# Sums over partitions by transposes and a VectorE sum, and identity products as transposes, in a two-layer hybrid decoder kernel

## The chip, the cores and the metric

The kernel runs on one core of one Trainium2 chip. The metric is the device time of one execution in microseconds (us). Three timed runs of the kernel before took 2297.41, 2301.21 and 2301.37 us, so the median is 2301.21 us.

Five engines matter. TensorE (PE in the profile, with its weight loads listed apart as PEld) multiplies matrices and writes to PSUM. VectorE (DVE) and ScalarE (ACT) do elementwise work and read PSUM. GpSimd (POOL) hardly works here. SyncE (SP) issues the transfers (DMA). Each engine takes its instructions in the order in which they were written into its queue.

## The reference, cut to what matters

Two decoder layers run over 1024 tokens of width 1024. Layer 0 has sparse attention, layer 1 a gated short convolution, and each is followed by a SwiGLU FFN. Everything is float32.

```python
c_act = jax.nn.silu(c)
for i in range(DEPTH):
    mod = c_act @ ada_w[i] + ada_b[i]
    sh1, sc1, g1, sh2, sc2, g2 = [m[:, None, :] for m in jnp.split(mod, 6, axis=-1)]
    h = _rmsnorm(x, norm1_g[i]) * (1.0 + sc1) + sh1
    ...                       # y = sparse attention (i = 0) or short convolution (i = 1) of h
    x = x + g1 * y
    h = _rmsnorm(x, norm2_g[i]) * (1.0 + sc2) + sh2
    x = x + g2 * _swiglu(h, ffn_w_gate[i], ffn_w_up[i], ffn_w_down[i])
return x
```

Three small things inside it are what the change touches: the vector-matrix product `c_act @ ada_w[i]` that gives the twelve conditioning vectors of 1024 values (six per layer), the sum of squares of each token in `_rmsnorm`, and the division by a per-token number (the norm's root, the key norm, the softmax's sum).

## The kernel before, in words

Activations lie transposed on the chip: features on the 128 partitions, tokens along the free side, in two halves of 512 tokens. A per-token number is therefore needed on every partition, and a sum over features is a sum over partitions.

**Large products.** Each float32 operand is split into a high and a low part (`whi`, `wlo`; ScalarE casts, VectorE subtracts), and every product is three matmuls, 128x128 weights against 512 columns (`mm3`). The FFN and the convolution's products use a two-by-two scheme with seven products instead of eight. Accumulators are PSUM banks of 128x512 float32: tags `mm` (2 banks), `g` (5 banks, in the part after attention), `o` (1), `L` (2 of two banks each, in attention) and `sm` (1 bank).

**Conditioning vectors.** `ada_step` multiplies a 128-row piece of `ada_w` by the 128 matching values of `c_act`, one per partition, and adds it into an accumulator (`acc` and `sc` for the first two vectors of layer 0, `adacc` for the others, 512 columns at a time). After eight pieces the accumulator has to be summed over its 128 partitions and turned so that a feature lies on a partition: `ada_end` does this with one float32 matmul per 128 columns, the accumulator as weights against a column of ones (`self.ones`), and VectorE adds `ada_b`. The first two vectors are made before the first norm. Ten halves (five vectors) are made during attention, eight during the first FFN, two during the second.

**Norms.** `norm_stat` squares x on ScalarE, adds the eight pieces on VectorE, and sums over partitions with four matmuls against ones, so that a token lies on a partition. `norm_bc` takes the root of 4 values per partition (`rsqrt_small`: VectorE, ScalarE, VectorE) and spreads them back: four float32 products with the identity, the weights being one value per partition repeated along 128 columns. The result is a 128x512 bank in which each partition has the norm factors of 512 tokens. There are six such statistics behind attention; the first norm of all gets its sums from ScalarE and uses `norm_bc` only.

**Attention.** For each block of 128 queries and each of 4 key groups: scores on PE into `ps_L`, mask and maximum on VectorE, exponent on ScalarE, transposes of the weights on PE (`p` against the identity, into an `mm` or `sm` bank), copies on ScalarE or VectorE (`pf`), values on PE into `ps_o`. `group_end` then divides by the softmax's sum: the reciprocal is repeated along 128 columns (`rw`) and turned by two products with the identity. `k_out` does the same for the key norm with four (`rb`), twice in all.

**What sets the order.** No engine order is written by hand. All calls are recorded with a priority, an estimate of their duration (`Plan.cost`) and their dependences, and `Plan.drain` writes them out engine by engine, as a list scheduler: whichever engine is free first takes the ready operation of the best priority. So an operation with another estimate can shift its neighbours. A tile of a tag with one buffer (`sm`) is handed on when all operations on the former tile are done. In the estimates a `transpose` counts 0.107 us of PE, and a float32 matmul with up to 128 columns 0.213 us.

In the profile every instruction has line 244 (the one place where recorded calls are written out), so tile names tell them apart.

Of the kernel before, what the change touches and what calls it, by code (L numbers as in the profile page):

```python
# [9 lines left out]
F32 = mybir.dt.float32  # L10
# [5 lines left out]
ALU = mybir.AluOpType  # L16
AX = mybir.AxisListType
# [433 lines left out]
P = 128  # L451
T = 1024
D = 1024
KT = D // P
TB = T // P
HW = 512
# [26 lines left out]
def blk(b):  # L483
    return slice(b * P, (b + 1) * P)


class Trunk:
# [97 lines left out]
    def setup(self, c, positions, ada_b, n1, n2, conv_w, gq, gk, lg, lb, rope_c, arenas, kgb, freq):  # L585
        nc, cp = self.nc, self.cp
# [3 lines left out]
                                fill=0.0, base=0, channel_multiplier=1)  # L590
        self.ones = cp.tile([P, 1], F32, name="ones")
        nc.vector.memset(self.ones, 1.0)
        self.blk4 = cp.tile([P, 4], F32, name="blk4")
# [57 lines left out]
    def ada_end(self, layer, j, lhs, half=0):  # L651

        nc = self.nc
        ps = self.ps("sm")
        n = 0
        for v in lhs:
            for c in range(0, v.free, P):
                nc.tensor.matmul(ps[:, n:n + 1], v[:, c:c + P], self.ones, start=True, stop=True)
                n += 1
        dst = self.mod[layer][j]  # L660
        c0 = half * 4
        b0 = layer * 48 + j * 8 + c0
        nc.vector.tensor_tensor(dst[:, c0:c0 + n], ps[:, 0:n], self.adab[:, b0:b0 + n],
                                op=ALU.add)
        if j in (1, 4) and c0 + n == KT:
            self.ada_scale(layer, j)
# [11 lines left out]
    def norm_bc(self, ss, sp, tag):  # L678
        nc = self.nc
# [3 lines left out]
        bc = self.ps(tag)  # L683
        for t in range(4):
            nc.tensor.matmul(bc[:, blk(t)], r[:, t:t + 1].to_broadcast([P, P]),
                             self.ident, start=True, stop=True)
        return bc
# [108 lines left out]
class Attention:  # L796
# [281 lines left out]
    def k_out(self, ab, rk, half, sl):  # L1078
# [5 lines left out]
        for i in range(4):  # L1084
            nc.tensor.matmul(bc[:, blk(i)], rb[:, blk(i)], tk.ident, start=True, stop=True)
        for two in range(2):
# [232 lines left out]
    def group_end(self, b, g, ops, sums):  # L1319
# [8 lines left out]
        for i in range(2):  # L1328
            nc.tensor.matmul(bc[:, blk(i)], rw[:, blk(i)], tk.ident, start=True, stop=True)
        on = sp.tile([P, 2, P], F32, name="on", tag="on")  # L1330
# [24 lines left out]
class Tail:  # L1355
# [57 lines left out]
    def norm_stat(self, half, tag="sm"):  # L1413
# [3 lines left out]
        for d in range(KT):  # L1417
# [4 lines left out]
            acc = sq  # L1422
        ss = self.tk.ps(tag)
        for t in range(4):
            nc.tensor.matmul(ss[:, t:t + 1], acc[:, blk(t)], self.tk.ones, start=True, stop=True)
        return self.tk.norm_bc(ss[:, 0:4], self.up, tag)

# [448 lines left out]
```

## Time and profile before

| | us |
|---|---|
| timed runs, lowest / median / highest | 2297.41 / 2301.21 / 2301.37 |
| profiled execution, span from first to last instruction | 2296.5 |
| PE busy | 2229.7 (97%), 11659 matmul instructions |
| VectorE busy | 1896.1 (83%), 3821 instructions |
| ScalarE busy | 1126.0 (49%), 2139 instructions |
| mean granted TensorE clock | 0.989 |

For the profiled execution only the span is recorded; the median of the timed runs lies 4.7 us (0.2%) above it. Differences worked out from the trace are made against the span and then set against the median.

PE is recorded as busy from an instruction's start to its result, and consecutive matmuls overlap, so the distance between starts tells what a matmul takes of the queue, and its duration does not. VectorE's and ScalarE's rows overlap a little too.

### The profile page before, as it was taken

How to read it: one execution, taken by the hardware profiler on the slowest of the kernel's cores; microseconds unless marked ns; L12 is line 12 of the kernel's file. 1: busy time of each engine (PE TensorE's matmuls, PEld its weight loads, DVE VectorE, ACT ScalarE, POOL GpSimd, SP SyncE). 2: the span in 40 equal slices, each digit the busy share in tenths (PEclk: the TensorE clock that was granted, in tenths of full speed). 3: DMA queues.
4: the chain of work that ended last, by engine and by line, in shares of the span. 5: the costliest groups of instructions: out<-in, count | busy, mean ns of one | idle time of the engine just before them, and what ended most of it. 6: DMA issues, size and time to landing. Idle time of an engine off the chain costs nothing.

```text
span 2296.5 us, 32967 instructions
## 1 busy us (share of the span) xinstructions
PE 2229.7 (97%) x11659; PEld 1803.9 (79%) x11659; DVE 1896.1 (83%) x3821; ACT 1126.0 (49%) x2139; POOL 5.5 (0%) x19
## 2 busy tenths in 40 slices
PE   5999999899999999999999999999999999999999
PEld 4757876777798878888888888778888888888887
DVE  7879999777679898878787899896898877767974
ACT  5577899756655333333444562224453333334444
POOL 0000000000000000000000000000000000000000
PEclk6999999999999999999999999999999999999999
DMA  9314333443335675545993354334346532349824
GB/s 318 119 55 108 87 109 103 129 130 101 120 113 145 185 237 174 178 129 170 341 332 108 99 147 129 115 96 156 117 132 203 163 119 88 124 133 377 294 85 138
DMA packets 334192, 356.37 MB, mean 155 GB/s; under 512 B 18090, under 2 KB 218827, under 8 KB 334027
## 3 DMA queue, kind: packets, MB, share of 16 engines
q1 hardware_dynamic: 333816, 354.14, 48.6%
q8 instruction: 91, 1.49, 0.3%
q14 instruction: 75, 0.61, 0.1%
q10 hardware_dynamic: 210, 0.14, 0.0%
HBM read 282.64 MB, written 71.57 MB: 154 GB/s over the span
## 4 chain that ended last, share of the span: by engine, by line
PE 53%; DVE 4%; DMA 3%; issue 1%; ACT 0%; ACTq 0%; SPq 0%; DVEq 0%
PE ps_g L244 36%; PE ps_mm L244 15%; PE ps_sm L244 3%; DMA raw<-in_conv_w_in_dram 2%; DVE u L244 1%; DVE wlo L244 1%; DVE s L244 1%; DVE v L244 1%; DMA ph<-in_ffn_w_down_dram 1%; ACT whi L244 0%; DVE xr L244 0%; DMA row10t<-cv 0%; DMA raw<-in_conv_w_out_dram 0%; DMA adaw<-in_ada_w_dram 0%; DMA s<-hid 0%
## 5 line engine op out<-in xcount | busy, mean ns | idle before, releaser
L244 ACT CAST whi<-raw 128x512 fp32r<-128x512 f32 (+1 forms) x306 | 187.0, 618 | 381.2 <-PE ps_g L244 149.1
L244 PE MATMUL ps_g<-t,whi 128*128 128x512 f32 x1184 | 365.4, 390 | 0.3 <-ACT whi L244 0.3
L244 ACT CAST whi<-s 128x512 fp32r<-128x512 f32 x276 | 171.0, 621 | 350.3 <-PE ps_g L244 153.9
L244 PE MATMUL ps_g<-h,whi 128*128 128x512 f32 x1056 | 326.2, 390 | 0.0
L244 DVE TENSOR_TENSOR wlo<-raw,whi 128x512 fp32r<-128x512 f32 (+1 forms) x314 | 213.7, 685 | 88.6 <-ACT whi L244 87.9
L244 PEld LDWEIGHTS ps_g<-t,whi 128*128 128x128 f32 x1184 | 221.8, 188 | 46.6 <-ACT whi L244 1.0
L244 PE MATMUL ps_g<-t,wlo 128*128 128x512 f32 x592 | 230.9, 390 | 0.1
L244 PEld LDWEIGHTS ps_g<-h,whi 128*128 128x128 f32 x1056 | 197.7, 188 | 40.6 <-ACT whi L244 0.2
L244 PE MATMUL ps_g<-h,wlo 128*128 128x512 f32 x528 | 206.1, 390 | 2.1 <-DVE wlo L244 2.1
L244 DVE TENSOR_TENSOR wlo<-s,whi 128x512 fp32r<-128x512 f32 x276 | 188.2, 684 | 18.1 <-ACT whi L244 17.6
L244 PE MATMUL ps_mm<-t,whi 128*128 128x512 f32 x608 | 187.6, 389 | 0.0
L244 PE MATMUL ps_g<-ph,whi 128*128 128x512 f32 x572 | 176.7, 389 | 0.0
L244 PEld LDWEIGHTS ps_mm<-t,whi 128*128 128x128 f32 x608 | 114.0, 188 | 23.8 <-DVE t L244 0.2
L244 PEld LDWEIGHTS ps_g<-t,wlo 128*128 128x128 f32 x592 | 111.2, 188 | 24.9 <-DVE wlo L244 1.8
L244 PEld LDWEIGHTS ps_g<-ph,whi 128*128 128x128 f32 x572 | 107.4, 188 | 22.2
L244 ACT ACTIVATE p<-p,nm,qsc 128x128 f32<-128x128 f32 (+7 forms) x128 | 112.1, 878 | 20.4 <-DVE nm L244 19.0
L244 DVE SCALAR_TENSOR_TENSOR adacc<-adaw,cact,adacc 128x512 f32<-128x512 f32 x140 | 104.4, 746 | 18.0 <-DMA adaw<-in_ada_w_dram 17.4
L244 DVE CUSTOM_DVE_ANT_0 p<-ps_L,bias 128x512 f32<-128x512 f32 (+3 forms) x192 | 99.6, 551 | 23.1 <-PE ps_mm L244 11.3
L244 PE MATMUL ps_mm<-t,wlo 128*128 128x512 f32 x304 | 118.5, 390 | 0.1
L244 ACT ACTIVATE junk<-sc,bs 128x896 bf16<-128x896 f32 (+3 forms) x124 | 109.7, 885 | 16.8 <-DVE bs L244 11.8
L244 PEld LDWEIGHTS ps_g<-h,wlo 128*128 128x128 f32 x528 | 99.1, 188 | 24.0 <-DVE wlo L244 3.4
L244 DVE TENSOR_TENSOR u<-u 128x512 f32<-128x512 f32 x170 | 114.2, 684 | 1.9 <-ACT u L244 0.8
(340 smaller groups left out, 4837.5 us busy)
## 6 DMA issues: line engine op xcount, KB each, us to landing
adaw<-in_ada_w_dram SPq DMA_DIRECT2D x160, 256.0 KB
ph<-in_ffn_w_down_dram SPq DMA_DIRECT2D x66, 512.0 KB
raw<-in_ffn_w_gate_dram SPq DMA_DIRECT2D x54, 512.0 KB
raw<-in_ffn_w_up_dram SPq DMA_DIRECT2D x54, 512.0 KB
raw<-in_conv_w_in_dram SPq DMA_DIRECT2D x34, 512.0 KB
raw<-in_ffn_w_down_dram SPq DMA_DIRECT2D x44, 256.0 KB
ph<-in_ffn_w_down_dram SPq DMA_DIRECT2D x44, 256.0 KB
raw<-in_attn_w_in_dram SPq DMA_DIRECT2D x18, 512.0 KB
```

The source lines that it names most:

```text
L244: f(*[a.get() if isinstance(a, Ref) else a for a in args], **{k: a.get() if isinstance(a, Ref) else a for k, a in kw.items()})
```

## The change

Two replacements are made, and nothing else is edited.

1. Products with the identity (in `norm_bc`, `k_out` and `group_end`) become `transpose` calls on the same operands and into the same places in PSUM.
2. Sums over partitions (in `ada_end` and `norm_stat`) no longer multiply by ones. Four transposes put the 128x512 accumulator, turned block by block, into a whole PSUM bank, and one VectorE `tensor_reduce` sums each 128 columns into one, giving 128x4 in SBUF. In `ada_end` the addition of `ada_b` follows as a second small VectorE instruction; for the first two vectors (1024 columns) this is done twice, through two successive `sm` tiles. `self.ones` goes.

The scheduler's estimates for the new calls are those of its rules (`transpose` 0.107 us, `tensor_reduce` 0.07 us + 1.04 ns per element), so the order of other instructions can move.

```diff
-        self.ones = cp.tile([P, 1], F32, name="ones")
-        nc.vector.memset(self.ones, 1.0)
...
     def ada_end(self, layer, j, lhs, half=0):
         nc = self.nc
-        ps = self.ps("sm")
-        n = 0
+        dst = self.mod[layer][j]
+        c0, b0 = half * 4, layer * 48 + j * 8
         for v in lhs:
-            for c in range(0, v.free, P):
-                nc.tensor.matmul(ps[:, n:n + 1], v[:, c:c + P], self.ones, start=True, stop=True)
-                n += 1
-        dst = self.mod[layer][j]
-        c0 = half * 4
-        b0 = layer * 48 + j * 8 + c0
-        nc.vector.tensor_tensor(dst[:, c0:c0 + n], ps[:, 0:n], self.adab[:, b0:b0 + n],
-                                op=ALU.add)
-        if j in (1, 4) and c0 + n == KT:
+            for c in range(0, v.free, HW):
+                ps = self.ps("sm")
+                for i in range(4):
+                    nc.tensor.transpose(ps[:, blk(i)], v[:, c + i * P:c + (i + 1) * P],
+                                        self.ident)
+                d = dst[:, c0:c0 + 4]
+                nc.vector.tensor_reduce(d, ps.rearrange("p (a b) -> p a b", b=P), axis=AX.X,
+                                        op=ALU.add)
+                nc.vector.tensor_tensor(d, d, self.adab[:, b0 + c0:b0 + c0 + 4], op=ALU.add)
+                c0 += 4
+        if j in (1, 4) and c0 == KT:
             self.ada_scale(layer, j)
...
         bc = self.ps(tag)
         for t in range(4):
-            nc.tensor.matmul(bc[:, blk(t)], r[:, t:t + 1].to_broadcast([P, P]),
-                             self.ident, start=True, stop=True)
+            nc.tensor.transpose(bc[:, blk(t)], r[:, t:t + 1].to_broadcast([P, P]), self.ident)
         return bc
...
         for i in range(4):
-            nc.tensor.matmul(bc[:, blk(i)], rb[:, blk(i)], tk.ident, start=True, stop=True)
+            nc.tensor.transpose(bc[:, blk(i)], rb[:, blk(i)], tk.ident)
...
         for i in range(2):
-            nc.tensor.matmul(bc[:, blk(i)], rw[:, blk(i)], tk.ident, start=True, stop=True)
+            nc.tensor.transpose(bc[:, blk(i)], rw[:, blk(i)], tk.ident)
...
-        ss = self.tk.ps(tag)
+        ps, ss = self.tk.ps(tag), self.up.tile([P, 4], F32, name="nss", tag="nss", bufs=2)
         for t in range(4):
-            nc.tensor.matmul(ss[:, t:t + 1], acc[:, blk(t)], self.tk.ones, start=True, stop=True)
-        return self.tk.norm_bc(ss[:, 0:4], self.up, tag)
+            nc.tensor.transpose(ps[:, blk(t)], acc[:, blk(t)], self.tk.ident)
+        nc.vector.tensor_reduce(ss, ps.rearrange("p (a b) -> p a b", b=P), axis=AX.X, op=ALU.add)
+        return self.tk.norm_bc(ss, self.up, tag)
```

The change moves instructions at two places of which the prediction speaks. The first is VectorE's queue ahead of the first norm. `acc` is the accumulator of the shift vector (the last of the two that are needed), `mod` the finished vectors, `zs` and `nz` the first norm's products, `wlo` a weight's low part, `hlo` the low part of the layer's input. Before:

```order
L244 SCALAR_TENSOR_TENSOR acc<-s_490,cact,acc 128x1024
L244 SCALAR_TENSOR_TENSOR zs<-xt,aff,ps_L 128x512
L244 SCALAR_TENSOR_TENSOR acc<-stage_397,cact,acc 128x1024
L244 TENSOR_TENSOR wlo<-raw,whi 128x288 x2
L244 SCALAR_TENSOR_TENSOR zs<-xt,aff,ps_L 128x512 x6
L244 TENSOR_TENSOR mod<-ps_sm,adab 128x8
L244 SCALAR_TENSOR_TENSOR zs<-xt,aff,ps_L 128x512
L244 SCALAR_TENSOR_TENSOR nz<-xt,aff,ps_L 128x512
```

And now, from the last step of the same accumulator on:

```order
L244 SCALAR_TENSOR_TENSOR acc<-stage_395,cact,acc 128x1024
L244 TENSOR_TENSOR wlo<-raw,whi 128x288
L244 SCALAR_TENSOR_TENSOR zs<-xt,aff,ps_L 128x512 x3
L244 TENSOR_REDUCE mod<-ps_sm 128x4
L244 SCALAR_TENSOR_TENSOR zs<-xt,aff,ps_L 128x512
L244 TENSOR_TENSOR mod<-mod,adab 128x4
L244 SCALAR_TENSOR_TENSOR zs<-xt,aff,ps_L 128x512 x2
L244 TENSOR_REDUCE mod<-ps_sm 128x4
L244 SCALAR_TENSOR_TENSOR zs<-xt,aff,ps_L 128x512
L244 TENSOR_TENSOR mod<-mod,adab 128x4
L244 SCALAR_TENSOR_TENSOR zs<-xt,aff,ps_L 128x512
L244 SCALAR_TENSOR_TENSOR nz<-xt,aff,ps_L 128x512
```

The vector is finished behind seven of the eight `zs` as before, but two sums of a whole bank now stand among them. Two more such sums, for the scale vector, stand further ahead between the steps of `acc`.

The second place is PE's queue at the last of the six norm statistics behind attention (second FFN, second half of the tokens). `nr` are the roots, the products with the identity spread them; the other rows are the FFN's products. Seven FFN matmuls stand between the sums of squares and the first row shown, before and now. Before:

```order
L244 MATMUL ps_g<-h_15266,whi 128x512 x2
L244 MATMUL ps_g<-h_15266,wlo 128x512
L244 MATMUL ps_mm<-h_15236,whi 128x512
L244 MATMUL ps_sm<-ident,nr 128x128 x4
L244 MATMUL ps_mm<-h_15236,whi 128x512
```

And now, from the matching row on:

```order
L244 MATMUL ps_g<-h_15300,whi 128x512 x2
L244 MATMUL ps_g<-h_15300,wlo 128x512
L244 MATMUL ps_mm<-h_15270,whi 128x512 x2
L244 MATMUL ps_mm<-h_15270,wlo 128x512
L244 MATMUL ps_mm<-h_15270,whi 128x512 x2
L244 MATMUL ps_mm<-h_15270,wlo 128x512
L244 MATMUL ps_mm<-h_15270,whi 128x512
L244 MATMUL ps_sm<-ident,nr 128x128 x4
L244 MATMUL ps_mm<-h_15270,whi 128x512
```

The spreading moved back by six FFN matmuls: 17 of them now stand between the sums and it, where 11 stood. In the other statistics it moved in the same direction, and at the conditioning vectors behind attention the four instructions stand where the four before stood, or a few matmuls later. From the last of these vectors on, PE's queue is the same as before.

## The prediction

> **What bounds the kernel now.** I read the busy time by stage first, then the chain that ended last, then PE's waits, then timelines of single operations. The columns are: stretch and its length, then busy us and instructions of PE, PEld, VectorE, ScalarE, GpSimd, granted clock, DMA share and GB/s.
>
> ```profile
> 0.00:50.00 50.00, 24.14 (x115) 20.09 (x115) 37.88 (x80) 24.03 (x40) 1.76 (x13) 0.69 0.92 315
> 50.00:300.00 250.00, 240.80 (x1246) 182.75 (x1247) 223.30 (x620) 181.51 (x386) 3.74 (x6) 0.97 0.37 105
> 300.00:400.00 100.00, 95.43 (x801) 64.86 (x800) 96.97 (x368) 97.36 (x267) 0.00 (x0) 0.98 0.33 96
> 400.00:640.00 240.00, 227.78 (x2035) 175.43 (x2035) 172.84 (x505) 157.19 (x312) 0.00 (x0) 1.00 0.37 115
> 640.00:1300.00 660.00, 657.26 (x3084) 549.42 (x3083) 562.99 (x930) 269.74 (x460) 0.00 (x0) 1.00 0.58 188
> 1300.00:1640.00 340.00, 334.04 (x1476) 273.25 (x1475) 294.04 (x503) 134.84 (x232) 0.00 (x0) 1.00 0.43 127
> 1640.00:2080.00 440.00, 440.00 (x1958) 364.93 (x1957) 354.01 (x577) 164.60 (x278) 0.00 (x0) 1.00 0.46 144
> 2080.00:2296.00 216.00, 210.27 (x955) 173.16 (x953) 154.05 (x245) 96.70 (x169) 0.00 (x0) 1.00 0.63 214
> ```
>
> ```profile
> PE 53%; DVE 4%; DMA 3%; issue 1%; ACT 0%; ACTq 0%; SPq 0%; DVEq 0%
> ```
>
> From 640 us on PE is busy for 1641.6 of 1656 us, and the last chain, which the profile follows back to 870 us, is PE nearly throughout. A microsecond of PE's queue taken away here is a microsecond of the kernel, unless VectorE (82% busy there) is then late. Before 50 us VectorE is the busier one. From 300 to 400 us ScalarE and VectorE are at 97%. From 400 to 640 us nobody is full: PE, VectorE and ScalarE hand work to one another.
>
> **What one group of four costs on PE.** First the four products with ones, then four with the identity, then four transposes (those of the output), each between 512-column matmuls at full clock; the columns are start, length, engine, line, operation.
>
> ```profile
> 1652.86 0.95 PE L244 MATMUL ps_sm<-ones,u 128*128 128x1 f32 x8
> 1653.67 0.47 PE L244 MATMUL ps_g<-h,wlo 128*128 128x512 f32 x1
> 1653.99 0.39 PE L244 MATMUL ps_g<-h,whi 128*128 128x512 f32 x1
> ```
>
> ```profile
> 683.09 0.39 PE L244 MATMUL ps_g<-h,whi 128*128 128x512 f32 x1
> 683.32 1.05 PE L244 MATMUL ps_sm<-ident,nr 128*128 128x128 f32 x8
> 684.12 0.48 PE L244 MATMUL ps_g<-h,whi 128*128 128x512 f32 x1
> 684.44 0.39 PE L244 MATMUL ps_g<-h,wlo 128*128 128x512 f32 x1
> ```
>
> ```profile
> 2273.61 0.60 PE L244 MATMUL ps_sm<-ident,xr 128*128 128x128 f32 x4
> 2273.96 0.48 PE L244 MATMUL ps_g<-whi 128*128 128x512 f32 x1
> 2274.28 0.39 PE L244 MATMUL ps_g<-wlo,whi 128*128 128x512 f32 x1
> ```
>
> A float32 product is two matmul instructions (x8 for four), a transpose one (x4 for four). A 512-column matmul takes 0.23 us from start to start (683.09 to 683.32). From the group's start to the second matmul behind it, less that 0.23: 1.13 - 0.23 = 0.90 us for ones, 1.12 - 0.23 = 0.89 for the identity, 0.67 - 0.23 = 0.44 for transposes. So a group of four saves **0.45 us of PE**, whichever kind it was, a pair in `group_end` about 0.22.
>
> [...]
>
> **How many, and where.** Groups with ones by stretch (instructions; eight are a group), and the rows of the others:
>
> ```profile
> 300.00:400.00 100.00, 2.00 (x16) 1.94 (x16) 0.00 (x0) 0.98 0.33 96
> 400.00:640.00 240.00, 8.01 (x64) 7.82 (x64) 0.00 (x0) 1.00 0.37 115
> 640.00:2296.00 1656.00, 15.46 (x128) 16.35 (x128) 0.00 (x0) 1.00 0.52 167
> ```
>
> ```profile
> L244 PE MATMUL ps_mm<-ident,rw 128*128 128x128 f32 x104 | 17.2, 289 | 0.3 <-ACT pf L244 0.3
> L244 PE MATMUL ps_sm<-ident,nr 128*128 128x128 f32 x40 | 5.5, 280 | 1.5 <-DVE nr L244 1.5
> L244 PE MATMUL ps_sm<-ident,rw 128*128 128x128 f32 x24 | 4.2, 296 | 0.2 <-DVE mod L244 0.2
> L244 PE MATMUL ps_o<-ident,rb 128*128 128x128 f32 x16 | 2.3, 284 | 0.0
> L244 PE MATMUL ps_g<-ident,nr 128*128 128x128 f32 x8 | 1.1, 274 | 0.0
> ```
>
> Behind attention: 16 groups with ones and 6 with `nr`. In attention: 2 + 8 groups with ones, and 32 pairs `rw` (128 instructions), 16 on either side of 400 us. Before it: 2 groups `rb`. In the head four groups with ones and two with `nr`, at half clock.
>
> **What is added.** A sum of 128x512 on VectorE for each group with ones: 6 for norms, 20 + 4 for vectors, 30 in all. None from PSUM stands in the trace; bounds are a 512-element sum from SBUF and a 512-element copy from PSUM. In `ada_end` a small addition stays, and the two in the head become four.
>
> ```profile
> L244 DVE TENSOR_REDUCE ln_v<-sc 128x8 f32<-128x512 f32 x1 | 0.7, 681 | 0.0
> L244 DVE COPY xt<-ps_mm 128x512 f32<-128x512 f32 x8 | 5.5, 687 | 5.5 <-PE ps_mm L244 5.4
> L244 DVE TENSOR_TENSOR mod<-ps_sm,adab 128x4 f32<-128x4 f32 x20 | 3.1, 154 | 0.0
> ```
>
> I take 0.68 us: 30 x 0.68 = 20.4 us more on VectorE, against some 25 us less on PE (56 groups, counting two pairs as one, x 0.45). Which of the two counts differs by stage.
>
> **Behind attention: -9.3 us.** 22 groups x 0.45 = 9.9 off PE's queue. The 16 sums put 10.9 us on VectorE, whose 1365 of 1656 us leave room. Queued behind each sum are the `wlo` subtractions, for which PE waits little today:
>
> ```profile
> PE ps_g L244 <- DVE wlo L244: 2.1, 3, 1.3
> PE ps_sm L244 <- DVE nr L244: 1.5, 2, 1.2
> PE ps_mm L244 <- DVE wlo L244: 1.3, 1, 1.3
> ```
>
> At a norm statistic the roots come 0.68 - 0.15 = 0.5 us later, but the spreading stands further back in PE's queue (17 instead of 11 matmuls, 1.4 us, at the place shown with the change), so PE does not wait for it. If all cover went, the sums would cost 10.9 and the gain would be gone; the worst stretch is 1300 to 1640 (VectorE 86%, three statistics near it). I take 0.6 us back.
>
> **Attention: -2.8 us.** Up to 400 us VectorE and ScalarE set the pace: 16 pairs and two groups off PE (4.5 us) bring nothing, two sums cost 1.4. Behind 400 us PE loses 16 x 0.22 + 8 x 0.45 = 7.2 us and VectorE, at 72%, hides its eight sums. PE's rows there are not free of waits, so I take two thirds, 4.7. The one `sm` bank, which the transposes of `p` use in turn, is held until the sum is done instead of a 0.15 us addition, 8 x 0.5 = 4 us at most; I take 0.5. Bounds: all 11.7 gained at no cost, or nothing gained and ten sums paid, +6.8.
>
> **Before it: -0.7 us.** Two groups `rb` with PE 96% busy, 0.9 us.
>
> **Head: +2.7 us.** Here the change loses. VectorE is in one piece of work without a gap until the shift vector is there, and ScalarE and then PE wait for that vector:
>
> ```profile
> 43.41 1.28 DVE L244 SCALAR_TENSOR_TENSOR acc<-stage,cact,acc 128x1024 f32<-128x1024 f32 x1
> 44.61 0.82 DVE L244 TENSOR_TENSOR wlo<-raw,whi 128x288 fp32r<-128x288 f32 x2
> 44.84 3.54 PE L244 MATMUL ps_sm<-ones,acc 128*128 128x1 f32 x16 [6.17 <-DVE acc L244]
> 45.35 4.03 DVE L244 SCALAR_TENSOR_TENSOR zs<-xt,aff,ps_L 128x512 f32<-128x512 f32 x6
> 49.30 0.16 DVE L244 TENSOR_TENSOR mod<-ps_sm,adab 128x8 f32<-128x8 f32 x1
> 50.27 0.70 PE L244 MATMUL ps_mm<-hhi,whi 128*72 128x512 f32 x1 [1.89 <-ACT hhi L244]
> ```
>
> The eight products with ones (3.54 us, twice what two groups cost later) lie under `zs`, so shortening them brings nothing. By the new order the same seven `zs` stand ahead of the vector, plus four sums and two small additions. At 0.6 to 0.68 us each (overlapped starts or full length) and 0.15: 2.4 to 2.7 and 0.2 to 0.3; I take 2.7. PE's first layer matmul should start near 53 instead of 50.3 us. If a transfer sets the pace in between, it is nearer 1.
>
> **Sum.** 2.7 - 0.7 - 2.8 - 9.3 = -10.1 us: span 2286.4, and with the 4.7 us by which the median lies above the profiled span, **2291.1 us**, 0.44% faster. 0.2% (4.6 us) is about what a measurement here tells from no change.
>
> **Rivals.** *Attention pays in full.* In attention PE waits for the held `sm` bank and for sums: nothing gained, ten sums paid. 2.7 - 0.7 + 6.8 - 9.3 = -0.5: 2300.7. For it: VectorE and ScalarE at 97% up to 400 us; against it: 72% and 65% behind. *Everything is gained.* Head hidden, attention in full: -0.9 - 11.7 - 9.9 = -22.5: 2278.7. Against it: VectorE has no gap in the head. *VectorE becomes the bound (slower).* Each sum waits in VectorE's queue for transposes that PE reaches late, and the `wlo` behind it are late for PE, behind attention too: 2.7 + 6.8 - 0.7 + (10.9 - 9.9) = +9.8: 2311.0. It decides once more than about two thirds of the sums' time reaches PE; against it, the waits for VectorE quoted above are 5 us in 1656. *The change doesn't do what it says*: a transpose of float32 would also be two instructions. The x4 above speaks against it.
>
> *The clock falls.* PE's granted clock is low in the head (0.69 on average), and a group takes twice as long there. If each of the 22 groups behind attention let it fall for 3 us, 1.5 us each would be lost, 33 in all: 2291.1 + 33 = 2324. Against it: the clock is 1.00 from 400 to 640 us, where most of these transposes run.
>
> ```profile
> L244 PE MATMUL ps_mm<-ident,p 128*128 128x128 f32 x368 | 62.4, 283 | 2.7 <-ACT pf L244 1.0 <-ACT p L244 0.8 <-DVE pf L244 0.6
> ```
>
> [...]
>
> **How the numbers follow.** Forecast 0.64; attention pays in full 0.17; everything gained 0.08; VectorE the bound 0.08; no saving or clock 0.03. The forecast's own range is 2284 to 2297. For eight in ten I take 2280 to 2303, which takes in the two milder rivals. Faster by over 0.2%: 0.72; within 0.2%: 0.18; slower: 0.10.
>
> **What would show it.** PE matmul instructions fall by 448 - 224 = 224. Groups `ones` become `ident` x4, about 0.44 us each. 30 TENSOR_REDUCE rows of about 680 ns. First `hhi` matmul near 53 us. The stretch behind attention 9 us shorter. The forecast is wrong if PE's waits for `wlo` or `nr` grow by more than some 5 us, if a sum from PSUM takes much over 0.68 us, or if attention gets longer.

## The result: 1.5% slower, and the profile after

The changed kernel takes 2331.7 us (median of four runs, 2328.7 to 2336.0) against 2299.3 us before on the same chip. The ratio is 1.0146, with a 95% interval of 1.0130 to 1.0161. The forecast was 2291.1 us, so 41 us are to be explained. The profiled run took 2336.0 us, its span is 2334.2.

What the prediction said of the count and the length of the new instructions came true. These are groups of the changed kernel (line, engine, operation, count, then busy us and mean ns of one, then idle time ahead):

```profile
L244 DVE TENSOR_REDUCE mod<-ps_sm 128x4 f32<-128x512 f32 x24 | 16.5, 686 | 0.1
L244 PE MATMUL ps_sm<-ident,adacc 128*128 128x128 f32 x80 | 12.4, 278 | 0.9 <-DVE adacc L244 0.9
```

And this is one group behind attention in its timeline:

```profile
1675.47 0.60 PE L244 MATMUL ps_sm<-ident,u 128*128 128x128 f32 x4
1675.83 0.48 PE L244 MATMUL ps_g<-h,wlo 128*128 128x512 f32 x1
1676.14 0.62 PE L244 MATMUL ps_g<-h,whi 128*128 128x512 f32 x2
```

Twenty groups with `adacc` are 80 instructions, a sum takes 0.686 us (forecast 0.68), and a group takes 1676.14 - 1675.47 - 0.23 = 0.44 us of PE (forecast 0.44). PE has 11435 matmul instructions, 224 fewer. What went wrong shows in the stages of the changed kernel (columns as in the prediction):

```profile
0.00:50.00 50.00, 21.42 (x89) 15.76 (x90) 36.87 (x78) 23.58 (x39) 1.76 (x13) 0.65 0.88 309
50.00:300.00 250.00, 233.89 (x1172) 175.31 (x1172) 218.95 (x594) 176.03 (x373) 2.88 (x6) 0.95 0.35 99
640.00:1300.00 660.00, 653.74 (x2974) 530.92 (x2973) 559.14 (x916) 259.07 (x443) 0.00 (x0) 1.00 0.56 186
1640.00:2080.00 440.00, 438.68 (x1888) 351.70 (x1887) 353.85 (x577) 163.66 (x276) 0.00 (x0) 1.00 0.42 130
```

From 1640 to 2080 us PE is busy nearly all the time (438.68 of 440 us) and at full clock, as before. But it gets through 1888 matmuls where it got through 1958, although the change touches hardly anything there. A hundred microseconds in which PE does nothing but 512-column products makes it plain. First the kernel before, then the change (busy us and instructions of PE, PEld, VectorE, ScalarE, GpSimd):

```profile
1940.00:2040.00 100.00, 100.00 (x443) 82.84 (x442) 74.83 (x120) 32.63 (x55) 0.00 (x0) 1.00 0.32 101
```

```profile
1940.00:2040.00 100.00, 100.00 (x430) 80.35 (x429) 73.27 (x117) 31.26 (x53) 0.00 (x0) 1.00 0.34 111
```

443 matmuls against 430: 3% fewer. The groups of one operation say the same. This is `ps_g<-ph,whi` before and after (ns: shortest, median, longest):

```profile
L244 PE MATMUL ps_g<-ph,whi x572: 389/389/398, 1109.1 to 2225.1; 128*128 128x512 f32 x191
```

```profile
L244 PE MATMUL ps_g<-ph,whi x572: 393/396/399, 1126.8 to 2262.7; 128*128 128x512 f32 x191
```

Even the shortest of the changed kernel is longer than the median before. This is no stall here and there, but every product.

**How the times were taken apart.** The trace has PE's matmuls in program order, as many as the program has (11659 before, 11435 after, a float32 product counting as two). So each start-to-start time can be set beside the addresses that the built program gives the two operands in SBUF, the on-chip memory in which the tiles lie. Behind attention run 6936 products of 512 columns. In 6216 the moving operand (the one of 512 columns; the other, the weights, has a 128x128 LDWEIGHTS row of its own in the trace) is `h`, `ph`, `t`, `rt` or `rh`, in 720 it is `whi` or `wlo`. From one product's start to the next, leaving out intervals over 0.3 us, which are waits or stand in a stretch at half clock:

| | `h`, `ph`, `t`, `rt`, `rh` moving | `whi`, `wlo` moving |
|---|---|---|
| before | 226.9 ns | 227.5 ns |
| the change | 233.3 ns | 227.8 ns |

Only the first kind is slower, and only its operands had moved. The old `ones` tile took 32 bytes of each partition, the two new `nss` tiles take 64, and `nss` lies ahead of the pools of `h` and `t`. So these tiles start 32 bytes higher. The weights' tiles hang from the other end of SBUF and stayed.

### The profile page after: what moved, and what is told of

Read it like the earlier page. It is cut to its first block, busy times and chain, and to the rows that moved or that the text cites. A ratio compares the mean times of both kernels' runs of the same rounds, so it can differ in the third digit from the quotient of the medians.

```text
span 2334.2 us, 32524 instructions
## 1 busy us (share of the span) xinstructions
PE 2252.7 (97%) x11435; PEld 1777.3 (76%) x11435; DVE 1916.6 (82%) x3851; ACT 1125.7 (48%) x2140; POOL 4.6 (0%) x19
## 4 chain that ended last, share of the span: by engine, by line
PE 72%; DVE 12%; DMA 5%; ACT 4%; issue 2%; SPq 0%; ACTq 0%; POOLq 0%; DVEq 0%
PE ps_g L244 42%; PE ps_mm L244 22%; PE ps_sm L244 5%; DVE s L244 2%; DVE u L244 2%; DMA raw<-in_conv_w_in_dram 2%; DVE wlo L244 2%; PE ps_L L244 2%; DMA adaw<-in_ada_w_dram 2%; PE ps_o L244 2%; DVE p L244 1%; ACT p L244 1%; DVE sc L244 1%; ACT junk L244 1%; DVE adacc L244 1%
## 5 line engine op out<-in xcount | busy, mean ns | idle before, releaser
L244 PE MATMUL ps_g<-t,whi 128*128 128x512 f32 x1184 | 373.6, 397 | 1.8 <-DVE whi L244 1.8
L244 PE MATMUL ps_g<-h,whi 128*128 128x512 f32 x1056 | 332.7, 396 | 0.1
L244 ACT ACTIVATE p<-p,nm,qsc 128x256 f32<-128x256 f32 (+7 forms) x128 | 112.5, 883 | 22.1 <-DVE nm L244 17.0
L244 DVE CUSTOM_DVE_ANT_0 p<-ps_L,bias 128x512 f32<-128x512 f32 (+3 forms) x192 | 100.0, 552 | 20.5 <-PE ps_mm L244 10.9
```

The lines of the kernel that those rows point to most:

```text
L244: f(*[a.get() if isinstance(a, Ref) else a for a in args], **{k: a.get() if isinstance(a, Ref) else a for k, a in kw.items()})
```

## Experiments on the place of the tiles

**The change, moved by 32 bytes.**

```diff
+        cp.tile([P, 8], F32, name="pad")
         self.blk4 = cp.tile([P, 4], F32, name="blk4")
```

> The changed kernel with one unused tile of 32 bytes per partition where the ones tile stood. PE's order is the changed kernel's own; what differs is that xr, h, ph and t lie 32 bytes higher, so that in the 6216 products behind attention whose moving operand is h, ph, rt or t this operand starts at 32 mod 64, as in the kernel before, and not at 0 mod 64. Theory (place in SBUF): these products start every 0.2267 us and not every 0.2333, 6216 x 0.0064 = 40 us come back, 2292 us against 2300 before; the prediction's own sum (2291) is then seen bare. Rival (the transposes, or the 224 fewer instructions, leave TensorE slower): nothing changes, 2331 us, and the starts stay 0.2333 us apart.

Measured: 2315.0 us, ratio 1.0065 (1.0051 to 1.0079). The 6216 products start 229.4 ns apart. Place matters, since 17 us came back with no other edit, but "32 mod 64" (the remainder of the address divided by 64) was not the rule.

**The kernel before, moved by 32 bytes** (the same line).

> The kernel before with the same unused tile of 32 bytes and no other edit: every instruction as before, xr, h, ph and t 32 bytes higher, which takes the moving operands of 6216 products behind attention from 32 mod 64 to 0 mod 64. Theory (place in SBUF): 6216 x 0.0064 = 40 us slower, 2340 us, starts 0.2333 us apart except where whi or wlo are themselves the moving operand (720 products). Rival (it was the transposes): 2300 us as before, starts 0.2267 us apart.

Measured: 2327.6 us, ratio 1.0124 (1.0109 to 1.0138), with the same instructions in the same order as before:

```profile
1940.00:2040.00 100.00, 100.00 (x431) 80.31 (x429) 73.03 (x117) 31.86 (x54) 0.00 (x0) 1.00 0.36 115
```

233.3 ns a product, exactly as in the change. So the transposes have no part in the slower pace. It cost 28 us and not 40: the products took 40.0 us more, and the waits behind attention fell from 17.3 to 5.9 us.

**Four places in one run.**

```diff
+        if name in self.pads:          # "h21", "h22", "t1", "t2"
+            self.pads.remove(name)
+            (self.bp if name in self.FIRST else self.tp).tile([P, 8], F32, ...)
```

> The changed kernel with unused tiles of 32 bytes between its operand tiles, so that one run has moving operands at 0 (4008 products), 32 (672), 64 (768) and 96 mod 128 (1488); the weights stay at 96 mod 128. If what counts is 32 mod 64, those at 32 and 96 start 0.2267 us apart and those at 0 and 64 0.2333: 1440 products fewer in the slow pace than in the changed kernel, 9 us, 2322 us. If only the residue of the weights themselves, 96 mod 128, is fast: 5 us, 2327. If the place doesn't matter: 0.2333 everywhere, 2332.

Measured in a single run: 2331.5 us. Against weights at 96 mod 128, operands at 0 had 233.3 ns (`ph`), at 32 229.3, at 64 233.1, at 96 232.9, at 128 234.1. Neither of the two rules held. Operands at 96 mod 128 had 232.9 ns here and 226.9 in the kernel before, against weights at 96 both times, so the remainder by 128 doesn't settle the pace.

**`whi` moved, `wlo` not** (an unused 32-byte tile between the two, and three of the four above).

> As the staggered one, with whi moved by 32 bytes to 0 mod 64 and wlo left at 32 mod 64, so that each moving operand meets weights of both kinds. If the moving operand's own place decides: those at 32 mod 64 0.2267 us apart, those at 0 mod 64 0.2333, whatever the weights; some 2313 us. If it is a clash between the moving operand and the weights that are loaded meanwhile, so that like places are fast: operands at 0 mod 64 are fast with whi and slow with wlo, and those at 32 mod 64 the other way round; some 2316 us. The starts tell the two apart, not the time.

Measured in a single run: 2328.5 us. Behind attention no pairing of moving operand and weights with a hundred products or more was under 230 ns, and neither theory's pattern showed. Even `whi` and `wlo` as moving operands, at 227.5 before, needed 232.0.

**Operands up by 32, weights down by 96** (the unused tile above, and one of 96 bytes behind `wlo`).

> The kernel before, all instructions its own: its operands behind attention moved up by 32 bytes as in the slow run of the kernel before, and the weights' tiles moved down by 96, so that both lie at 0 mod 128. If like places are fast: 0.2270 us a product and 2300 us. If 0 mod 64 is slow for the moving operand whatever the weights: 0.2333 and 2328 us.

Measured in a single run: 2323.8 us, 232.4 ns a product, 227.7 for those with `whi` or `wlo` moving. Like places mod 128 aren't enough. But the distance from weights to moving operand is now 128, and operands 128 from their weights had 232.9 in the staggered run. In each run whose weights lie together, the distance mod 256 orders all the numbers.

**Operands lower than the weights.**

```diff
-        self.blk4 = cp.tile([P, 4], F32, name="blk4")
+        blk4 = cp.tile([P, 8], F32, name="blk4")
+        self.blk4, self.nss = blk4.part_of(0)[:, 0:4], blk4.part_of(1)[:, 4:8]
...
-        r = sp.tile([P, 4], F32, name="nr", tag="nr", bufs=2)
+        r = sp.tile([P, 4], F32, name="nr", tag="nr", bufs=1)
```

(and the pads ahead of `h21` and `t1`)

> The change with nss in the free half of the blk4 tile and one nr buffer instead of two, so that the operands lie lower against the weights: 1992 products have their moving operand 64 bytes below the weights mod 256 (a distance of 192), 1440 have it 32 below (224), 3504 at the same place. By the runs so far the start-to-start time hangs on the distance mod 256: 0.2270 us at 0, 0.2333 at 32, 0.2294 at 64, 0.233 at 96, 0.2325 at 128, 0.234 at 160. If the rule is symmetric about 0: 0.2333 at 224 and 0.2294 at 192, and (1440 x 6.3 + 1992 x 2.4) ns = 14 us over the change in place, 2317 us. If only the operand's own place counts (480 mod 512 fast): some 0.233 at both, 2325 us. If any place below is as good as 0: 2303 us.

Measured in a single run: 2322.7 us; 233.2 to 233.3 ns at distance 192, 233.2 at 224, 227.7 for `t` at distance 0 in the same run. Not symmetric: 192 is slow, 64 (229.4 ns in the change moved by 32 bytes) about half as much.

**Both moved by the same 32 bytes.**

```diff
+        blk4 = cp.tile([P, 8], F32, name="blk4")
+        self.blk4, self.ones = blk4.part_of(0)[:, 0:4], blk4.part_of(1)[:, 4:5]
...
+            self.wp.tile([P, 8], F32, name="padw", tag="padw", bufs=1)   # behind wlo
```

> The kernel before, all instructions its own and in its order, with the ones tile in the free half of the blk4 tile, so that xr, h, ph and t lie 32 bytes lower, and with the weights' tiles 32 bytes lower too: moving operands and weights both at 192 mod 256 instead of 224. If the distance of the two mod 256 sets the pace: 0.2270 us a product and 2300 us, as before. If the operand's own place does (224 mod 256 was fast, and 0, 32, 64, 96, 128, 160 and 192 were slow, though always against other weights): 0.233 us and some 2325 us.

Measured: 2297.6 us, ratio 0.9987 (0.9977 to 0.9996), 226.9 ns:

```profile
1940.00:2040.00 100.00, 100.00 (x442) 82.78 (x442) 73.48 (x117) 32.80 (x56) 0.00 (x0) 1.00 0.32 101
```

The operands lie at another address, their distance is 0 again, and the pace is the old one. So among the layouts run here with all weights at one residue, the pace goes by the distance:

| moving operand minus weights, mod 256 | 0 | 32 | 64 | 96 | 128 | 160 | 192 | 224 |
|---|---|---|---|---|---|---|---|---|
| ns from start to start | 226.9 to 227.7 | 233.3 | 229.4 | 233.1 | 232.4 to 232.9 | 234.1 | 233.3 | 233.2 |

Moving one operand against the other by 32 bytes changed the pace by 3% (226.9 to 233.3 ns), and moving both together did not (226.9), so the pace hangs on where the two lie to each other. Why it does no run shows. That the distance isn't the whole rule is shown by the run with `whi` and `wlo` 32 bytes apart, where even pairs at distance 0 were slow (`whi` against `whi` 232.5 ns). And at distance 64, in the change moved by 32 bytes, `h` against `wlo` had 228.5 ns and `ph` against `wlo` 232.1.

**The change with every tile in its old place.** `nss` takes the 32 bytes of the old `ones` tile; all else, and every engine's order, is the change's.

```diff
+        self.nss = cp.tile([P, 4], F32, name="nss")
...
-        ps, ss = self.tk.ps(tag), self.up.tile([P, 4], F32, name="nss", tag="nss", bufs=2)
+        ps, ss = self.tk.ps(tag), self.tk.nss
```

> The changed kernel with its nss tile, the sums of squares, in the 32 bytes where the ones tile stood, so that every other tile lies at the address of the kernel before; every engine's order is the changed kernel's own. Moving operands and weights are both at 96 mod 128 again. Theory (the pace hangs on where the moving operand lies against the weights, mod 128): 0.2270 us a product where the run moved by 32 had 0.2294 and the change 0.2333, (0.2294 - 0.2270) x 6193 = 15 us below the 2315 of the run moved by 32, 2300 us: the change bare is worth about nothing, 8 us lost ahead of attention, some 10 won in it, and the rest behind it. Rival (something in the change itself slows TensorE's products, the place only in part): 0.229 us a product, 2315 us.

Measured: 2303.5 us, ratio 1.0013 (1.0003 to 1.0024), 226.9 ns a product:

```profile
1940.00:2040.00 100.00, 100.00 (x443) 82.83 (x442) 73.52 (x118) 32.49 (x55) 0.00 (x0) 1.00 0.33 104
```

**28 of the 32 us lost are the place.** What is left of the change is +0.13%, and that is where the prediction's own terms are to be judged.

## Experiments on the change itself

The table has, for each kernel, the median; when PE does attention's first and last `rw` product or transpose; and the time behind attention (first product into `ps_g` to the last output transpose) in three parts. The column "small" is all matmuls under 512 columns: the groups of four, and 34.8 us of 256-column products that are the same in every row. "Products" are the 512-column products at their own pace, and "waits" is the rest. All in us, from one profile each.

| | median | first `rw` | last `rw` | small | products | waits | sum |
|---|---|---|---|---|---|---|---|
| before | 2299.3 | 310.7 | 626.6 | 59.0 | 1574.2 | 17.3 | 1650.5 |
| the change | 2331.7 | 321.3 | 631.2 | 49.3 | 1614.4 | 19.7 | 1683.5 |
| the change in place | 2303.5 | 321.2 | 627.8 | 49.3 | 1574.4 | 26.9 | 1650.6 |
| transposes alone | 2303.6 | 319.6 | 632.8 | 56.7 | 1574.1 | 19.9 | 1650.7 |
| sums alone | 2316.6 | 325.6 | 641.2 | 52.1 | 1574.4 | 27.9 | 1654.4 |
| head's sums as products | 2312.0 | 319.6 | 637.3 | 49.3 | 1574.4 | 33.1 | 1656.8 |
| transposes, order kept | 2297.0 | 309.9 | 625.8 | 56.1 | 1574.4 | 17.3 | 1647.8 |
| and 20 sums, order kept | 2300.9 | 312.8 | 631.8 | 51.3 | 1574.2 | 24.1 | 1649.7 |
| the same on ScalarE | 2308.1 | 312.4 | 641.6 | 51.4 | 1574.3 | 20.5 | 1646.2 |

The waits hold one thing more. Behind attention the granted clock stands at half for stretches of 3.4 us, in some profiles. There are none in the kernel before and with the transposes at the kept order. There is one each in the change (875.0 to 878.4 us), the change in place and the last two rows, and it costs 1.4 to 1.6 us. In the other three rows they add up to 10.2 us and cost 3.7 to 4.6.

Profiles of one and the same order differ too. From first to last `rw`, four of the kernel before (itself and its three moves) have 315.0 to 318.2 us, and six of the change 305.9 to 310.4. The waits of the kernel before were 17.3 us, and 19.1 with both moved by 32 bytes. Nor is the profiled run always near the median: with the transposes at the kept order it was the fastest of eleven (2295.0 us), with the head's sums as products the slowest of six (2315.2). So 2 or 3 us between two rows say little.

In place, the change takes 9.7 us of groups off PE behind attention (forecast 9.9) and puts 9.6 us of waits in their stead. Ahead of attention it loses 10.5 us, and attention's stretch is 9.3 us shorter. The runs below say why, as far as they can.

**The transposes alone** (tiles in place, sums as products).

```diff
-            nc.tensor.matmul(bc[:, blk(i)], rw[:, blk(i)], tk.ident, start=True, stop=True)
+            nc.tensor.transpose(bc[:, blk(i)], rw[:, blk(i)], tk.ident)
```

(the same for `rb` and `nr`)

> The kernel before with its identity products (the 16 groups of attention, 2 of the projection, 8 of the norms) as transposes; the sums stay products with ones, and all tiles stay where they were. By the prediction's own terms: attention 16 x 0.45 x 2/3 = 4.7 us, the two of the projection 0.7, the six groups behind attention 2.7: 2300 - 8 = 2292 us. If the loss ahead of attention (8 us in the change) is the sums', first products start as before and attention starts at 311 us; if it is the transposes', attention starts at 319.

Measured: 2303.6 us, ratio 1.0012 (1.0004 to 1.0020). The first `hlo` product is at 51.7 us (51.5 before), but attention starts 9 us late. The time goes in one stretch of the projection, first before, then in this run:

```profile
195.00:215.00 20.00, 20.00 (x101) 16.92 (x100) 19.84 (x69) 17.83 (x36) 0.00 (x0) 1.00 0.77 171
```

```profile
195.00:215.00 20.00, 17.52 (x72) 14.99 (x73) 15.85 (x50) 14.02 (x27) 0.00 (x0) 0.74 0.69 169
```

The gaps come first: between 190 and 197 us PE waits 3.1 us for ScalarE's `qsq` and 1.9 us for `wlo`. Then the granted clock stands at half from 197.0 to 207.3 us, which is its mean of 0.74 in this stretch.

**The sums alone** (identity products kept, tiles in place).

> The change without its transposes of identity products: only the sums over partitions are four transposes and one VectorE sum, all tiles in the place of the kernel before. By the prediction's terms: ahead of attention +2.7 us, attention +1.4 +0.5, behind it 16 groups x 0.45 = 7.2 us less: 2300 - 3 = 2297 us. By what the run moved by 32 showed (8 us lost ahead of attention, 8 us more of waiting for wlo and for operands behind it, at 830 to 880 us above all): 2300 + 8 - 7 + 8 = 2309 us, and attention starts at 319 us.

Measured: 2316.6 us, ratio 1.0066 (1.0051 to 1.0081). The first `hlo` product is at 54.4 us, and attention starts at 325.6, later than either reading expected. Behind attention 6.9 us of groups go and 10.6 us of waits come.

**The head's four sums left as products.**

```diff
+        if lhs[0].free > HW:           # the head's two vectors: 8 products with ones each
+            ...
+                    nc.tensor.matmul(ps[:, m:m + 1], v[:, c:c + P], self.ones, ...)
```

> The change with all tiles in the place of the kernel before, and with the four sums of the head (shift and scale vectors of the first layer, ahead of the projection) left as 16 products with ones; ones and nss share the 32 bytes of the old ones tile. If the loss ahead of attention is the head's four sums (2.7 us in the prediction, 10.5 us measured in the change in place): the first product with hlo starts at 51.5 us and not 54.5, attention at 311, 2303.5 - 10 = 2293 us. If it is the planner's new layout of the projection: the first hlo product at 51.5, but attention at 318 to 320 as with the transposes alone, 2301 us.

Measured: 2312.0 us, ratio 1.0043 (1.0029 to 1.0056). The first `hlo` product comes at 52.3 us, 2.1 earlier than in the change in place, but attention starts at 319.6, where the transposes alone also put it. So the head's sums cost some 2 to 3 us, and the rest of the 10 is the planner's new layout of the projection. Behind attention this run has 6 us more of waits than the change in place, and 3 of the 6 are its two further stretches at half clock.

**The transposes, with the order kept.** The planner costs a transpose at half a product, so new prices move everything behind. Here it goes on counting products, and transposes are issued in their places; every engine's order is the old one.

```diff
+    def turned(self, out, x, ident):
+        op = self.record("tensor", "matmul", (out, x, ident), {"start": True, "stop": True})
+        op.emit = self.emitter("tensor", "transpose", (out, x, ident), {})
```

> The kernel before with its 24 groups of identity products issued as transposes, but entered in the planner as the products that they were, so that every engine's order is that of the kernel before, row for row, and all tiles are in its places. Theory (the planner, which costs a transpose at 0.107 us and a product at 0.213, lays out the work ahead of attention anew, and that lost the 9 us there in the run of the transposes alone): attention starts at 310 us, 0.7 earlier than before, attention gives 4.7 us and the six groups behind it 2.7, as the prediction priced them: 2292 us. Rival (the loss is the transposes' own): attention starts at 319 us again, 2303 us.

Measured: 2297.0 us, ratio 0.9987 (0.9978 to 0.9996). Attention starts at 309.9, so the loss ahead of it was the order. Behind attention 2.7 us are gone, the price of six groups. **Attention itself got no shorter**: 315.9 us from first to last `rw` before, 315.8 now, with 64 products turned into transposes. The forecast of 2292 us is missed by that. PE may have had time to spare there. But the clock differs too:

```profile
310.00:627.00 317.00, 301.31 (x2643) 220.55 (x2640) 252.51 (x812) 238.52 (x541) 0.00 (x0) 1.00 0.37 114
```

```profile
310.00:627.00 317.00, 299.09 (x2577) 214.27 (x2578) 251.20 (x809) 238.05 (x538) 0.00 (x0) 0.98 0.37 114
```

From first to last `rw` the clock stood at half for 1.8 us before and for 12.5 us now. In such a stretch products start about 0.43 us apart instead of 0.23 (850 us in the change in place). So, as an estimate, up to (12.5 - 1.8) / 2 = 5.4 us of PE's time went that way, as much as the transposes were to save. Whether spare time or the clock took the gain, these profiles don't tell.

**Twenty sums on top, with the order kept,** first on VectorE, then on ScalarE.

```diff
+                if v.free == HW:
+                    op.emit = nc.emitter("tensor", "transpose", (ps[:, blk(n)], v[:, c:c + P], self.ident), {})
...
+            emits = [nc.emitter("vector", "tensor_reduce", ...), nc.emitter("vector", "tensor_tensor", ...)]
```

> The run with transposes at the kept order, and on top of it the 20 sums of the later conditioning vectors (10 in attention, 10 behind it) as four transposes and one VectorE sum, entered in the planner as the four products and the one addition that they were: every other instruction stays where it stood in the kernel before, and all tiles are in its places. If behind attention the sums' gain on TensorE's queue (10 x 0.45 = 4.5 us) was lost to the planner's new order: 2297 - 4.5 = 2292.5 us, waits of products for products at 29 us as in the run without the sums. If VectorE's 0.68 us a sum delays whi and wlo by as much as TensorE saves (it is 102 of 110 us busy from 790 to 900 us): 2297 us or a little more, the waits 5 us longer, most of it between 790 and 1050 us.

Measured: 2300.9 us, ratio 1.0005 (0.9996 to 1.0014), 3.8 us above the run without the sums. Behind attention 4.8 us of groups go and 6.8 us of waits come. (The 29 us of waits of this expectation and the next is another count of the run without the sums, which has 17.3 in the table.) This is VectorE's busiest stretch without the sums, then with them:

```profile
790.00:900.00 110.00, 106.38 (x474) 86.39 (x474) 100.45 (x171) 33.02 (x57) 0.00 (x0) 1.00 0.65 206
```

```profile
790.00:900.00 110.00, 103.19 (x454) 82.49 (x453) 101.06 (x170) 30.69 (x54) 0.00 (x0) 1.00 0.65 204
```

VectorE is about as busy, with as many instructions, although four sums are now among them: other work of its moved back. PE has 20 instructions fewer, 16 of them by the change itself, and 3.2 us less of busy time, where four groups account for 1.8.

```diff
+            emits = [nc.emitter("scalar", "activation", (ps[:, blk(i)], ps[:, blk(i)], AF.Identity),
+                                {"accum_out": dst[:, c0 + i:c0 + i + 1]}) for i in range(n)]
```

> The same with each sum as four ScalarE activations with an accumulated output in place of the one VectorE sum; VectorE then has exactly the instructions of the kernel before. ScalarE is busy 664 of 1650 us behind attention, and four such activations cost it some 1 us (an estimate from its 0.28 us for 128 columns). If VectorE's time was what ate the gain: 2297 - 4.5 = 2292.5 us, waits as without the sums (29 us). If the longer way of a sum itself (PSUM held, four instructions more before the vector is there) or the transposes cost it: 2297 us or more.

Measured: 2308.1 us, ratio 1.0038 (1.0026 to 1.0050). Behind attention it is the shortest of all, 1646.2: waits are 3.6 us lower than with VectorE's sums, though not down to 17.3. That speaks for VectorE's time as a part of the added waits; its size doesn't follow from one profile each. In attention it loses 13 us against the run without sums. ScalarE's part, and what VectorE waited for from 310 to 642 us:

```profile
L244 ACT ACTIVATE ps_sm<-ps_sm 128x128 f32<-128x128 f32 x80 | 21.1, 264 | 2.7 <-PE ps_sm L244 0.6
L244 ACT ACTIVATION_READ_ACCUMULATOR ps_sm<-ps_sm 128x1 f32 x80 | 15.6, 195 | 0.0
```

```profile
DVE mod L244 <- ACT ps_sm L244: 14.0, 9, 3.1
```

Each activation is followed by an instruction that reads the accumulated value, so a sum kept ScalarE busy for 1.40 us (1153.2 us in all against 1125.2 without the sums, over 20), not the 1 us expected. The small addition on VectorE, kept in its old place in the queue, stands there for 14 us until ScalarE is done, and all of VectorE's work behind it stands too.

No version beats the kernel before by more than the 0.13% of the kept order, and moving all operands and weights together by 32 bytes, which should change nothing, gave 0.13% as well.

## Why the prediction was wrong, step by step

**The change part by part: a step was missing.** It counted instructions, queues and waits, but not that one tile went and two came, and that all tiles behind them move. It took a 512-column product at 0.23 us before and after alike; the 6216 products went from 226.9 to 233.3 ns, 40 us in all, a part of which shorter waits took in. That term is worth +28 us, and no rival had it. The one that named a similar time, "the clock falls" (2324), was wrong in its cause: behind attention the clock stood at half once in the change, for 3.4 us, which cost 1.6 us and not 33.

**"What one group of four costs": right.** Forecast 0.45 us saved; 9.7 / 22 = 0.44 in the change in place. Instructions and the 0.68 us of a sum were right too.

**"Behind attention: -9.3": the 0.6 us taken back was the mistake.** With tiles in place the groups save 9.7 and the waits grow by 9.6 (1.6 of it at half clock), so the stage gives 0. The cover was read from the stage's mean, VectorE at 82%, and from its worst stretch as I thought, 1300 to 1640. The one that counted is 790 to 900 us, where VectorE was 93% busy (102.06 of 110) and where the first of eight sums come. First before, then in place:

```profile
790.00:900.00 110.00, 107.32 (x480) 87.53 (x479) 102.06 (x173) 33.33 (x57) 0.00 (x0) 1.00 0.66 209
```

```profile
790.00:900.00 110.00, 103.54 (x442) 81.94 (x441) 99.18 (x168) 31.41 (x53) 0.00 (x0) 0.98 0.64 202
```

By the 1000th product of the stage (913 us before, 918 in place) 6.5 of the 9.6 us had come. In all eight profiles with the sums at the planner's new order, 6 to 9 us of waits lie between the 700th and the 800th product (841 to 872 us in place). In the other eight it is 0.1 us at most, also at the kept order with the same eight sums, and with the transposes alone. So it took the sums and the order that the planner made with them.

The prediction's "if all cover went" (the gain would be gone) is the size that came out. Its own mark, waits for `wlo` or `nr` growing by more than 5 us, was not reached: they grew from 4.9 to 8.3 us. PE's longer waits in the change in place, behind 640 us, show these and new ones beside them (engine, tile, releaser, then us in total, times, longest):

```profile
PE ps_g L244 <- DVE wlo L244: 4.6, 8, 1.1
PE ps_mm L244 <- ACT whi L244: 2.7, 3, 1.4
PE ps_g L244 <- DVE whi L244: 2.6, 2, 1.4
PE ps_sm L244 <- DVE nr L244: 1.9, 1, 1.9
PE ps_mm L244 <- DVE wlo L244: 1.8, 3, 1.2
```

`wlo` grew from 3.4 us to 6.4, and `whi`, which VectorE makes too at some places, came in with 2.6. At the kept order the waits grew by 6.8 us with the sums on VectorE and by 3.2 with them on ScalarE, in both cases with 1.4 to 1.5 us of half clock among them. How much of the 9.6 us is VectorE's time and how much the new order was not told apart.

**"Attention: -2.8": a wrong price that something else covered.** The 4.7 us for PE's lighter load behind 400 us came out as 0 at the kept order, where the clock was also lower; why is open, as said there. In the change in place the stretch from first to last `rw` is 9.3 us shorter, but it starts 10.5 later; with the transposes or the sums alone it is 2.7 and 0.3 us shorter. That points to the planner shifting work over the border, and not to the operations; no run shows it by itself. From the start to the last `rw`, forecast -0.8 (2.7 - 0.7 - 2.8), measured +1.2.

**"Head: +2.7": right in mechanism and nearly in size.** In the change PE's first product with `hlo` waits for VectorE, and VectorE has the late sum and `zs` ahead of `hlo`. Before, then the change on PE, then the change on VectorE:

```profile
51.49 0.70 PE L244 MATMUL ps_mm<-hlo,whi 128*72 128x512 f32 x1 [0.52 <-DVE hlo L244]
```

```profile
51.00 0.70 PE L244 MATMUL ps_mm<-hhi,whi 128*72 128x512 f32 x1 [0.36 <-ACT hhi L244]
54.87 0.70 PE L244 MATMUL ps_mm<-hlo,whi 128*72 128x512 f32 x1 [3.17 <-DVE hlo L244]
```

```profile
51.42 0.69 DVE L244 TENSOR_REDUCE mod<-ps_sm 128x4 f32<-128x512 f32 x1
52.02 0.74 DVE L244 SCALAR_TENSOR_TENSOR zs<-xt,aff,ps_L 128x512 f32<-128x512 f32 x1
52.68 0.16 DVE L244 TENSOR_TENSOR mod<-mod,adab 128x4 f32<-128x4 f32 x1
52.75 0.75 DVE L244 SCALAR_TENSOR_TENSOR zs<-xt,aff,ps_L 128x512 f32<-128x512 f32 x1
```

54.87 against 51.49 us before, or 54.43 with tiles in place: 2.9 to 3.4 us. The first `hhi` product did not move to 53 as I wrote, probably since half of the vector is there early. What the step missed is behind it: the planner laid the projection out anew, and 7 us more were lost by the start of attention.

**"Before it: -0.7": in line with the kept order** (309.9 against 310.7, though the kernel before with its tiles moved also had 310.0 to 311.4), buried under the 10 us elsewhere.

**The rivals.** "VectorE becomes the bound" (2311) named waits for VectorE behind sums, which is a part of what took the gain behind attention, so 0.08 was too low a chance. "Everything is gained" fell with the head and the waits. Whether the transposes lower the clock in attention stays open: at the kept order the granted clock there is 0.98 where it was 1.00 before, but the kernel before moved by 32 bytes, without such transposes, has a dip at the same place (410 us), and with its operands up by 32 and its weights down by 96 it has 0.98 from 310 to 627 us too.

## What to carry to other kernels

An edit that adds or drops a tile moves every tile behind it, here by 32 bytes. Where a stage is nothing but back-to-back products, compare the addresses in the two built programs first, and hold them still (put the new tile into the old one's space) before judging the edit; at 6216 products, 6.4 ns each are 40 us. A gain on the busiest engine needs room on the engine that takes over the work (VectorE was 82% busy over the stage, 93% from 790 to 900 us), and that is better read in stretches of 100 us than of a whole stage. And where a planner orders the work, keep its prices while the operation is exchanged: here its new layout alone moved the start of attention by 9 us, about as much as the largest term of the change.

## What the runs showed of the hardware

- The start-to-start time of a 128x512 product of split operands (type float32r in the kernel) that changes weights from one to the next is 226.9 to 227.7 ns with the moving operand and the weights at the same SBUF address mod 256, and 229.4 to 234.1 ns at the seven other distances in steps of 32 bytes, as long as all weights have one address mod 256. It was 226.9 at two absolute places (224 and 192 mod 256).
- In the kernel before moved by 32 bytes, 40.0 us more of products came with 11.4 us less of waits behind attention, and the kernel was 28 us longer.
- A VectorE sum over 512 columns from PSUM to 4 values took 0.686 us; four ScalarE activations of 128 columns with accumulated outputs (0.264 us each) kept ScalarE busy for 1.40 us together, each followed by a read of the accumulator (0.195 us).
- Turning 64 products of attention into transposes, at the kept order, changed its length by 0.1 us in one profile each, with 12.5 us at half clock where there were 1.8.
- Stretches at half clock were 3.4, 6.8 and 30.7 us long in the profile before, and 3.4, 6.8, 13.7 and 30.7 in the change's. In the run of the transposes alone, 5.0 us of PE's waits between 190 and 197 us were followed by half clock from 197.0 to 207.3 us.
